# Five edits to a hybrid encoder trunk: unnormalised prompt rows, values stored whole, values between the chunks, gates loaded ahead of the merge

## The chip, the cores and the metric

One core of one Trainium2 chip runs the whole program. The metric is the device time of one launch in microseconds (us), the median of several runs. Times of single instructions come from one profiled execution, taken by the hardware profiler. The engines are TensorE (PE, matmuls; PEld is its weight load), VectorE (DVE), ScalarE (ACT), GpSimd (POOL) and SyncE (SP, which here issues every DMA, in order).

## The reference

One layer and a final norm, applied with the same weights to 512 prompt rows and 1024 sample rows of width 1024, in f32:

```
h = rms_norm(x, norm1_g)
z = h @ w_in                                   # branches and gates
br_a = conformer_conv(z_a)    br_b = multiscale_pool(z_b)    br_c = short_gated_conv(z_c)
br_d = neighbourhood_attention(q, k, v, rpb) @ w_out_d
gates = sigmoid(z_gates + b_gate)              # four gates of width 1024
x = x + (gates0 * br_a + gates1 * br_b + gates2 * br_c + gates3 * br_d) @ w_o
h = rms_norm(x, norm2_g)
x = x + conv_glu_ffn(h, w_up, ffn_conv_w, w_down)
return rms_norm(x, final_g)
```

RMSNorm multiplies each row by the reciprocal of its root mean square (one scalar for each row) and each column by a gain g.

## The kernel before

Activations are kept transposed: features on the 128 partitions, rows along the free axis, in chunks of C = 512 rows. Chunk c = 0 is the prompt, c = 1 and 2 the sample. A row of 1024 features is KT = 8 tiles of 128x512. A product in f32 is made of three matmuls of rounded halves (`mm3`, L121 to L125: high times high, high times low, low times high); `split` (L114, L115) makes the halves, the high one on ACT, the low one on DVE.

**Phase A** (L327 to L531) loads x, and makes the queries and keys (`zt`, four PSUM tiles a chunk) and the values (`zv`, four blocks `b` of 128 rows a chunk, `value_tile`). For the prompt the q/k and values are made from unnormalised rows `raw0` (x times gain), and the row scale goes in at eviction. For the sample `scale(c)` makes the row scale from the sum of squares (matmuls with `ones`, L142, then a small Newton chain on DVE, then the tile `dg`), `spread` (L156) spreads it over the partitions into `rb`, and `norm(k, c)` (L421) multiplies x by it, tile by tile. After q/k of both chunks come the values of chunk 1, with `operands(b)` (sums and differences of sample tiles T1 to T4, on DVE and POOL, stored to DRAM, for a Strassen-like product later), and the values of chunk 2. Between these last value blocks the prompt is loaded a second time (L338), multiplied by gain and row scale `rbp` (L529) and split into `h[0]`.

**Phase B** (L535 to L803) makes the branch projections (`ftile`: tiles `z2_1` for item 2 and chunk 1, and so on, chunk order 1, 2, 0) in a planned order; an attention task list (`bg`) is pumped between them. An attention `step` (24 of them: 2 head pairs, 3 row blocks, 4 column blocks `j`) loads its values `vv`, computes scores, softmax and `o`. Eviction functions `ev_...` take each z from PSUM.

**Gate phase** (L808 to L955): 16 pairs of gate columns, seven products a pair for the sample plus two for the prompt (`plain`), sigmoid, and a store to `gate_d` in DRAM. A side task (`step`, `tick`, TAPS = 5) runs the 31-tap convolution on DVE. At the end `load_bs(c)` loads the branch outputs of chunk c from DRAM (8 tiles `bs` of 128x512) and splits them into `bh` and `bl`.

**Merge** (L963 to L989): for feature tile d and chunk c, `merge(d, c, w)` loads a gate tile of 1 MB (`g`, L970), makes four products `y{d}{c}{i}` (6 matmuls each), multiplies each by its gate on DVE (L975), adds the four on POOL (L976, L977) and DVE (L978). The first two d are interleaved: (0,0), (1,0), (0,1), (1,1), (0,2), (1,2). Eight PSUM banks hold the y tiles.

A scheduler lays all of it out once, when the program is built, by priorities and due times; each engine then runs its own list in order and waits on semaphores. The output projection, the FFN and the final norm follow the merge and are not touched.

## Time and profile before

| what | value |
|---|---|
| median of 3 runs | 2275.09 us (2274.45 to 2275.87) |
| the profiled execution | 2275.41 us |
| its span, first to last instruction | 2273.6 us (1.81 us lie outside) |
| PE busy | 2199.9 us, 97% |
| DVE, ACT, POOL busy | 59%, 34%, 28% |
| mean granted TensorE clock | 0.983 of full speed |

The span less PE's busy time is 73.7 us: the idle time of PE in the whole program. A busy PE at the lower of its two clock levels (granted clock 0.50, which is 1.2 GHz against 2.4 GHz) takes twice as long for a matmul, so the rows carry the granted clock beside the busy time. "[3.83 <-DVE dg L147]" behind an instruction says that its engine had been idle for 3.83 us and that the DVE instruction of line 147, writing `dg`, released it.

### The profile page before, as it was taken

To read this page: it belongs to the slowest core of one execution; us is meant where nothing else is said; L and a number is where in the kernel's file an instruction comes from. 1 tells how busy PE (TensorE), PEld (TensorE's weight loads), DVE (VectorE), ACT (ScalarE), POOL (GpSimd) and SP (SyncE) were. 2 spreads that over 40 slices of the span, in tenths; PEclk is the share of its full clock that TensorE was granted. 3 is DMA by queue.
4 is the path that set the end of the run, shared out by engine and by line. 5 is a ranking of instruction groups with operands and counts; after the bars stand their busy time and mean duration, and the time that the engine had idled before them with its cause. 6 is when DMAs were issued, how large, how long until landed. Compare 5 with 4: busy or idle time off the path is not lost.

```text
span 2273.6 us, 26886 instructions
## 1 busy us (share of the span) xinstructions
PE 2199.9 (97%) x9898; PEld 1789.9 (79%) x9898; DVE 1351.8 (59%) x1946; ACT 781.3 (34%) x1328; POOL 632.4 (28%) x695
## 2 busy tenths in 40 slices
PE   8979999999999999799998999999999999999997
PEld 6767677888888887588786788888888888888886
DVE  6733554436555564677439897778878875341414
ACT  5325444333333333501223533333333333321112
POOL 3201424222222221144234353444444430000001
PEclk9999999999999999899999999999999999999999
DMA  6565232622233223775332321111111114532231
GB/s 214 183 219 175 90 115 68 229 88 93 88 103 102 83 80 111 243 248 194 116 122 101 120 75 61 58 59 65 65 62 60 65 66 167 174 119 59 77 92 51
DMA packets 115444, 259.13 MB, mean 114 GB/s; under 512 B 13168, under 2 KB 23920, under 8 KB 112240
## 3 DMA queue, kind: packets, MB, share of 16 engines
q1 hardware_dynamic: 115312, 257.41, 33.9%
q8 instruction: 78, 1.28, 0.2%
q14 instruction: 54, 0.44, 0.1%
HBM read 169.53 MB, written 87.83 MB: 113 GB/s over the span
## 4 chain that ended last, share of the span: by engine, by line
PE 49%; DVE 2%; issue 0%; POOL 0%; POOLq 0%; ACT 0%; DVEq 0%; ACTq 0%
PE yp L124 5%; PE yp L123 5%; PE yp L125 5%; PE ppu L125 3%; PE ppu L123 3%; PE ppu L124 3%; PE o L124 2%; PE o L123 2%; PE o L125 2%; PE p3T L125 1%; PE p3T L124 1%; PE p3T L123 1%; PE p1T L124 1%; PE p1T L125 1%; PE p1T L123 1%; PE p22T L125 1%
## 5 line engine op out<-in xcount | busy, mean ns | idle before, releaser
L123 PE MATMUL yp<-fs,wdhi 128*128 128x512 f32 x480 | 187.0, 391 | 0.0
L124 PE MATMUL yp<-fs,wdhi 128*128 128x512 f32 x480 | 186.9, 389 | 0.0
L125 PE MATMUL yp<-fs,wdlo 128*128 128x512 f32 x480 | 186.8, 389 | 0.0
L115 DVE TENSOR_TENSOR fs<-fr,fs 128x512 fp32r<-128x512 f32 x63 | 43.5, 691 | 181.8 <-ACT fs L114 181.7
L1173 POOL TENSOR_TENSOR u<-u,u 128x512 f32<-128x512 f32 x63 | 97.5, 1548 | 193.3 <-DVE u L1166 135.6
L123 PE MATMUL z<-hh,wh_i 128*128 128x512 f32 x288 | 120.1, 418 | 11.8 <-ACT hh L114 11.8
L837 DVE SCALAR_TENSOR_TENSOR acc<-glu,pt,acc 128x1552 f32<-128x1552 f32 x60 | 124.2, 2069 | 5.1 <-ACT acc L835 4.2
L124 PE MATMUL z<-hl,wh_i 128*128 128x512 f32 x288 | 116.4, 405 | 0.5 <-DVE hl L115 0.5
L125 PE MATMUL z<-hh,wl_i 128*128 128x512 f32 x288 | 115.7, 403 | 0.0
L1266 POOL TENSOR_TENSOR x<-x,rs 128x256 f32<-128x256 f32 x11 | 7.6, 723 | 366.1 <-DVE acc L1254 362.5
L114 ACT CAST fs<-fr 128x512 fp32r<-128x512 f32 x63 | 39.1, 621 | 199.0 <-DMA fr<-f_d 101.3
L123 PEld LDWEIGHTS yp<-fs,wdhi 128*128 128x128 f32 x480 | 90.1, 188 | 19.5 <-issue 0.5
L124 PEld LDWEIGHTS yp<-fs,wdhi 128*128 128x128 f32 x480 | 90.1, 188 | 19.0 <-issue 0.5
L125 PEld LDWEIGHTS yp<-fs,wdlo 128*128 128x128 f32 x480 | 90.1, 188 | 18.9
L1166 DVE SCALAR_TENSOR_TENSOR u<-c,pt,u 128x512 f32<-128x512 f32 x88 | 100.5, 1180 | 0.0
L123 PE MATMUL y<-bh,wh_wo 128*128 128x512 f32 x192 | 75.8, 395 | 16.2 <-DVE g L975 16.2
L614 POOL TENSOR_TENSOR bm<-R,pt 128x384 f32<-128x384 f32 (+1 forms) x48 | 47.3, 990 | 151.5 <-DVE mx L621 124.4
L1165 DVE SCALAR_TENSOR_TENSOR u<-c,pt,u 128x512 f32<-128x512 f32 x88 | 87.0, 1027 | 0.0
L253 POOL TENSOR_TENSOR Sg<-wr_g,wr_g 128x512 f32<-128x512 f32 x16 | 22.0, 1376 | 217.9 <-DVE Sg1s L115 217.9
L1172 ACT ACTIVATE u<-u 128x512 f32<-128x512 f32 x66 | 41.8, 633 | 111.9 <-DVE u L1166 111.9
L123 PEld LDWEIGHTS z<-hh,wh_i 128*128 128x128 f32 x288 | 55.3, 192 | 28.9 <-ACT hh L114 13.7
L124 PE MATMUL o<-ml,wh_o 128*128 128x512 f32 x192 | 75.6, 394 | 1.2 <-DVE ml L115 1.2
(498 smaller groups left out, 6493.7 us busy)
## 6 DMA issues: line engine op xcount, KB each, us to landing
g<-gate_d SPq DMA_DIRECT2D x24, 1024.0 KB, 5.2
wr_u<-in_w_up SPq DMA_DIRECT2D x44, 512.0 KB, 3.5
f_d<-u SPq DMA_DIRECT2D x66, 256.0 KB, 2.0
fr<-f_d SPq DMA_DIRECT2D x66, 256.0 KB, 2.7
wr_g<-in_w_in SPq DMA_DIRECT2D x32, 512.0 KB, 4.1
wdr<-in_w_dn SPq DMA_DIRECT2D x23, 512.0 KB, 3.5
x<-in_xT SPq DMA_DIRECT2D x32, 256.0 KB, 5.1
gate_d<-gp SPq DMA_DIRECT2D x32, 256.0 KB, 2.9
```

The lines of the kernel that those rows point to most:

```text
L114: S.copy(hi, src)
L115: V.tensor_tensor(lo, src, hi.bitcast(F32), ALU.subtract)
L123: PE.matmul(ps, w[0][:, ws], x[0], start=first, stop=False, **kw)
L124: PE.matmul(ps, w[0][:, ws], x[1], start=False, stop=False, **kw)
L125: PE.matmul(ps, w[1][:, ws], x[0], start=False, stop=last, **kw)
L253: G.tensor_tensor(t, x, y, op)
L614: G.tensor_tensor(bmv, rv, cm[:, None, :].broadcast_to([P, nk, 32]), ALU.add)
L837: keep(V.scalar_tensor_tensor(a, g, w, a, ALU.mult, ALU.add))
L1165: V.scalar_tensor_tensor(b, r[:, 0:C], pc("fc", f * 3), b, ALU.mult, ALU.add)
L1166: V.scalar_tensor_tensor(b, r[:, 2 : C + 2], pc("fc", f * 3 + 2), b, ALU.mult, ALU.add)
L1172: S.activation(ug, ug, AF.Silu)
L1173: (V if j == NJ - 1 else G).tensor_tensor(uv, uv, ug, ALU.mult)
```

## The change

1. The prompt stays unnormalised: `h[0]` is `raw0`. The second load of the prompt, its norm (8 DVE instructions at L529) and its 8 splits go. The row scale `rbp` (now in a pool that lives on) goes in at the eviction of each prompt tile instead.
2. The values of a block are stored by one DMA of 128 partitions, where 8 of 32 partitions were: 12 stores in place of 96. A step's `vv` is then loaded by four DMAs of 32 partitions, where one was: 96 in place of 24.
3. Values of chunk 1 stand between the q/k of chunk 1 and of chunk 2; the spread of chunk 2's row scale comes after value block 2 and its first two norms after block 3. `operands(b)` stand with the values of chunk 2.
4. The loads of `bs` for chunks 1 and 2 move behind the gate phase, into a pool of 4 tiles of their own, and the first three gate tiles (0,0), (1,0), (0,1) are loaded among them.
5. The gate pool has 9 tiles, and the sums S1 to S4 of the gate weights come from it, where they came from the T pool (TPN 34 to 32, TPA 40 to 39). The loop that ran the rest of the side task empty becomes an assertion; TAPS stays 5.

```diff
-            raw0 = {}
+            raw0 = [None] * KT
+            h[0] = raw0
...
-                    raw0[k] = hl(f"rh{k}"), hl(f"rl{k}")
+                    raw0[k] = pr[k] = hl(f"rh{k}"), hl(f"rl{k}")
...
-                for r in range(2):
-                    for j in range(4):
-                        lo = r * GW + CB[j]
-                        SP.dma_start(vt_d[j, c * 8 + b * 2 + r], o[lo : lo + 32, :].bitcast(F32))
+                SP.dma_start(vt_d[2 * (c * 4 + b) : 2 * (c * 4 + b) + 2].rearrange("r c d -> (r c) d"), o.bitcast(F32))
...
             for c in (1, 2):
+                zz = [ztile(f"zt{c}{n}") for n in range(4)]
...
                 for b in range(4):
                     value_tile(c, b, h[c])
-                    if c == 1:
+                    if c == 1 and b == 2:
+                        spread(*stat[2][:2])
+                    if c == 1 and b == 3:
+                        with tc.high_priority():
+                            norm(0, 2)
+                            norm(1, 2)
+                    if c == 2:
                         operands(b)
-                    else:
-                        for k in (2 * b, 2 * b + 1):
-                            load_x(k, 0)
-                            keep(V.scalar_tensor_tensor(x[k, 0], x[k, 0], pc("g1", k), rbp, ALU.mult, ALU.mult))
-                            h[0][k] = pr[k] = hl(f"hh{k}_0"), hl(f"hl{k}_0")
-                            split(*h[0][k], x[k, 0])
...
-                        SP.dma_start(
-                            vv[:, :nt].bitcast(F32),
...
+                        for r in range(4):
+                            SP.dma_start(
+                                vv[r * 32 : (r + 1) * 32, :nt].bitcast(F32),
...
                     def ev_g(c, z):
                         sig[c] = go(f"sig{i}{c}")
+                        if c == 0:
+                            V.tensor_tensor(sig[c], z, rbp, ALU.mult)
+                            z = sig[c]
                         S.activation(sig[c], z, AF.Sigmoid)
+                        if c == 0:
+                            G.tensor_tensor(sig[c], sig[c], rbp, ALU.mult)
...
+                        if c == 0:
+                            V.tensor_tensor(o, z, rbp, ALU.mult)
+                            G.tensor_tensor(o, o, rbp, ALU.mult)
+                        else:
+                            S.copy(o, z)
...
+                        o = cc[:, OFF[0] : OFF[0] + C]
+                        G.tensor_tensor(o, o, rbp, ALU.mult)
...
                     z = prompt(n, s, wg)
-                    gate_out(*gate, 0, z, go(f"gp{s}{n}"))
+                    o = go(f"gp{s}{n}")
+                    V.tensor_tensor(o, z, rbp, ALU.mult)
+                    gate_out(*gate, 0, o, o)
...
             for _ in step:
-                pass
-            load_bs(1)
-            load_bs(2)
+                raise AssertionError
...
+                    bst = pool(p2a, "bst", 4, side="right")
+                    load_gate(0, 0)
+                    load_bs(1)
+                    load_gate(1, 0)
+                    load_gate(0, 1)
+                    load_bs(2)
```

Where the instructions stand now. **First place, PE after the q/k of chunk 1**, where the row scale of chunk 2 is made (`rb0_2`; `zt2.` are q/k of chunk 2, `zv1.` and `zv2.` values). Before:

```order
L142 MATMUL rb0_2_874<-ones_168,sq0_24_812 128x1
L156 MATMUL rb0_2_874<-dg0_2_875,ones_168 128x512
L123 MATMUL zt20_924<-hh0_2_929,wh_q0_186 128x512
L123 MATMUL zt21_925<-hh0_2_929,m0h0_259 128x512
L123 MATMUL zt22_926<-hh0_2_929,wh_k0_189 128x512
L123 MATMUL zt23_927<-hh0_2_929,m1h0_277 128x512
L460 MATMUL zv10_1088<-vwh0_316,hh0_1_645 128x256
```

After:

```order
L142 MATMUL rb0_2_849<-ones_168,sq0_24_787 128x1
L463 MATMUL zv10_898<-vwh0_320,hh0_1_627 128x256
...
L465 MATMUL zv12_956<-vwh3_323,hl7_1_830 128x256
L156 MATMUL rb0_2_849<-dg0_2_850,ones_168 128x512
L463 MATMUL zv13_986<-vwh0_320,hh0_1_627 128x256
...
L465 MATMUL zv13_986<-vwh3_323,hl7_1_830 128x256
L123 MATMUL zt20_1025<-hh0_2_1016,wh_q0_190 128x512
L123 MATMUL zt21_1026<-hh0_2_1016,m0h0_263 128x512
```

Three value blocks (72 matmuls of 256 columns) now stand between the sum of squares and the spread, and one (24) between the spread and the first product of chunk 2.

**Second place, SP at the end of phase A**: the value stores (`vt_d`), the second load of the prompt (`x0_0` and on), the operand stores (`t_d`) and the first loads of phase B (`wr_i3`, `qh0`). Before:

```order
L519 DMA t_dT43_119<-T4l3_1342 128x512
L473 DMA vt_d_103<-vs20_1373 32x512 x8
L338 DMA x0_0_1384<-in_xT 128x512
L338 DMA x1_0_1391<-in_xT 128x512
L473 DMA vt_d_103<-vs21_1423 32x512 x8
...
L338 DMA x7_0_1541<-in_xT 128x512
L202 DMA wr_i3_1668<-in_w_in 128x1024
L202 DMA wr_i4_1765<-in_w_in 128x1024
L656 DMA qh0_1755<-qh_d0_95 128x1536
```

After:

```order
L473 DMA vt_d_103<-vs22_1320 128x512
...
L473 DMA vt_d_103<-vs23_1378 128x512
L497 DMA t_dT13_107<-T1l3_1388 128x512
...
L497 DMA t_dT43_119<-T4l3_1406 128x512
L202 DMA wr_i3_1533<-in_w_in 128x1024
L202 DMA wr_i4_1630<-in_w_in 128x1024
L650 DMA qh0_1620<-qh_d0_95 128x1536
```

The prompt loads are gone, a value block is one row where it was eight, and the operand stores of the last tiles stand right ahead of the phase B loads.

**Third place, DVE at the start of the merge** (`bl` is the low half of a branch tile, `g00` the gate tile of d = 0, c = 0, multiplied by the products `y`). Before:

```order
L115 TENSOR_TENSOR wl_wo1_7807<-wr_wo1_7805,wh_wo1_7806 128x1024
L115 TENSOR_TENSOR bl001_7703<-bs001_7700,bh001_7702 128x512
L115 TENSOR_TENSOR bl011_7709<-bs011_7706,bh011_7708 128x512
...
L115 TENSOR_TENSOR bl312_7793<-bs312_7790,bh312_7792 128x512
L975 TENSOR_TENSOR g00_7819<-y000_7821,g00_7819 128x512
```

After:

```order
L115 TENSOR_TENSOR wl_wo1_7791<-wr_wo1_7789,wh_wo1_7790 128x1024
L999 TENSOR_TENSOR g00_7687<-y000_7803,g00_7687 128x512
L999 TENSOR_TENSOR g00_7687<-y001_7811,g00_7687 128x512
L999 TENSOR_TENSOR g00_7687<-y002_7819,g00_7687 128x512
L115 TENSOR_TENSOR bl001_7692<-bs001_7689,bh001_7691 128x512
L999 TENSOR_TENSOR g00_7687<-y003_7827,g00_7687 128x512
L115 TENSOR_TENSOR bl011_7698<-bs011_7695,bh011_7697 128x512
L115 TENSOR_TENSOR bl101_7704<-bs101_7701,bh101_7703 128x512
L1002 TENSOR_TENSOR m0_7801<-g00_7687 128x512
L115 TENSOR_TENSOR bl111_7710<-bs111_7707,bh111_7709 128x512
L999 TENSOR_TENSOR g10_7737<-y100_7838,g10_7737 128x512
```

All 16 low halves stood ahead of the first gate product; now the gate products come first and the low halves between them. SP's list at this place, before:

```order
L818 DMA gate_d7_64<-gr15_7697 128x512
L890 DMA bs001_7700<-bs_d001_121 128x512
...
L890 DMA bs312_7790<-bs_d312_143 128x512
L970 DMA g00_7819<-gate_d0_57 128x2048
L970 DMA g10_7856<-gate_d1_58 128x2048
```

After:

```order
L828 DMA gate_d7_64<-gr15_7672 128x512
L982 DMA g00_7687<-gate_d0_57 128x2048
L902 DMA bs001_7689<-bs_d001_121 128x512
L902 DMA bs011_7695<-bs_d011_124 128x512
L902 DMA bs101_7701<-bs_d101_127 128x512
L902 DMA bs111_7707<-bs_d111_130 128x512
L982 DMA g10_7737<-gate_d1_58 128x2048
L902 DMA bs201_7713<-bs_d201_133 128x512
...
L902 DMA bs311_7731<-bs_d311_142 128x512
L982 DMA g01_7739<-gate_d0_57 128x2048
L902 DMA bs002_7741<-bs_d002_122 128x512
```

The first gate load stands right behind the last gate store, and each later `bs` load reuses the slot of the fourth `bs` load before it.

## Rows read from the trace of the kernel before

**Rows 1.** PE's waits: engine, line, waited for: us in total, times, longest us

```profile
PE y L123 <- DVE g L975: 16.2, 1, 16.2
PE z L123 <- ACT hh L114: 11.8, 3, 10.1
PE rb L156 <- DVE dg L147: 6.8, 3, 3.8
PE tp L633 <- ACT se L630: 4.1, 10, 0.7
```

**Rows 2.** Windows: us, PE PEld DVE ACT POOL busy (instructions), PEclk, DMA share, GB/s

```profile
85.00:90.00 5.00, 3.92 (x14) 3.54 (x15) 5.00 (x9) 2.47 (x4) 1.28 (x1) 0.50 0.07 25
150.00:200.00 50.00, 43.20 (x169) 32.12 (x170) 18.56 (x35) 15.76 (x26) 3.23 (x7) 0.83 0.76 253
250.00:300.00 50.00, 48.86 (x246) 35.49 (x244) 23.60 (x65) 25.80 (x59) 19.84 (x21) 1.00 0.36 122
450.00:500.00 50.00, 50.00 (x223) 41.39 (x222) 19.83 (x23) 20.14 (x31) 10.99 (x7) 1.00 0.30 88
955.00:960.00 5.00, 3.35 (x8) 2.71 (x9) 3.27 (x6) 0.00 (x0) 2.52 (x2) 0.50 0.97 408
1220.00:1225.00 5.00, 3.12 (x14) 2.04 (x12) 5.00 (x6) 1.24 (x2) 4.92 (x3) 1.00 0.22 64
```

**Rows 3.** Timeline at chunk 2's row scale, PE then DVE: start, us, instruction [idle before]

```profile
82.51 2.08 PE L156 MATMUL rb<-dg,ones 128*128 128x512 f32 x2 [3.83 <-DVE dg L147]
86.08 0.80 PE L123 MATMUL zt<-hh,wh_q 128*128 128x512 f32 x1 [1.49 <-ACT hh L114]
91.58 0.30 PE L462 MATMUL zv<-vwh,hl 128*128 128x256 f32 x1
91.71 0.28 PE L460 MATMUL zv<-vwh,hh 128*128 128x256 f32 x1
84.62 5.36 DVE L421 SCALAR_TENSOR_TENSOR x<-x,pg,rb 128x512 f32<-128x512 f32 x8 [1.57 <-PE rb L156]
119.33 0.68 DVE L115 TENSOR_TENSOR T4l<-x,T4h 128x512 fp32r<-128x512 f32 x1
```

**Rows 4.** Timeline at the first projections, PE, DVE, SP

```profile
133.45 0.40 PE L123 MATMUL z<-hh,wh_i 128*128 128x512 f32 x1
154.58 0.80 PE L123 MATMUL z<-hh,wh_i 128*128 128x512 f32 x1 [10.06 <-ACT hh L114]
185.70 0.39 PE L123 MATMUL z<-hh,wh_i 128*128 128x512 f32 x1
153.13 0.75 DVE L529 SCALAR_TENSOR_TENSOR x<-x,pg,rbp 128x512 f32<-128x512 f32 x1 [18.65 <-DMA x<-in_xT]
146.22 4.04 SPq L473 DMA_DIRECT2D vt_d<-vs  x8
```

**Rows 5.** Timeline at the start of the merge, PE, DVE, SP

```profile
940.04 0.39 PE L125 MATMUL y<-bh,wl_wo 128*128 128x512 f32 x1
956.65 0.77 PE L123 MATMUL y<-bh,wh_wo 128*128 128x512 f32 x1 [16.23 <-DVE g L975]
939.37 5.38 DVE L115 TENSOR_TENSOR bl<-bs,bh 128x512 fp32r<-128x512 f32 x8 [8.50 <-ACT bh L114]
933.08 12.02 SPq L890 DMA_DIRECT2D bs<-bs_d  x16
950.70 14.15 SPq L970 DMA_DIRECT2D g<-gate_d  x5
```

**Rows 6.** DMA issues from 905 to 980 us: instruction, count, KB each, median us to landing

```profile
g<-gate_d SPq DMA_DIRECT2D x8, 1024.0 KB, 5.3
bs<-bs_d SPq DMA_DIRECT2D x23, 256.0 KB, 4.3
```

**Rows 7.** Attention stage, 190 to 450 us: a value load; POOL's and ACT's instructions by line

```profile
vv<-vt_d SPq DMA_DIRECT2D x16, 384.0 KB, 3.2
L614 POOL TENSOR_TENSOR bm<-R,pt 128x384 f32<-128x384 f32 x32 | 33.0, 1034 | 79.8 <-DVE mx L621 79.8
```

More of the change, by code (lines that the diff above doesn't have):

```diff
@@ L42 @@
 TAPS = 5
-TPA = 40
-TPN = 34
+TPA = 39
+TPN = 32
 NBIG = 9
@@ L325, in tt @@
             return tp.tile([P, C], dt, tag="t", name=name)
+        rbp = pool(outer, "rbp", 1).tile([P, C], F32, name="rbp")
         with ExitStack() as pha:
@@ L729, in ev_gc @@
                             t["gc"] = big(f"gc{i}")
-                        S.copy(t["gc"][:, ch(c)], z)
+                        o = t["gc"][:, ch(c)]
+                        if c == 0:
+                            V.tensor_tensor(o, z, rbp, ALU.mult)
+                            G.tensor_tensor(o, o, rbp, ALU.mult)
+                        else:
+                            S.copy(o, z)
                     def ev_xv(c, z):
@@ L785, in encoder @@
                 early = Weights([(w_in[idx], f"i{idx}") for idx, _ in todo])
-                wg = PairWeights("g", lambda n: tuple(w_in[gate_idx(*g)] for g in pairs[n]), lambda name: tt(name))
+                wg = PairWeights("g", lambda n: tuple(w_in[gate_idx(*g)] for g in pairs[n]), lambda name: go(name))
                 left = len(todo)
@@ L810, in encoder @@
             cvp = pool(phb, "cvp", 2, side="right")
-            go1 = pool(phb, "gob", 8, side="right")
+            go1 = pool(phb, "gob", 9, side="right")
             def go(name, dt=F32):
@@ L888, in load_bs @@
                     for k in range(2):
-                        t = go(f"bs{i}{k}{c}")
+                        t = bst.tile([P, C], F32, tag="go", name=f"bs{i}{k}{c}")
                         SP.dma_start(t, bs_d[i, k, c])
@@ L965, in encoder, with load_gate @@
                     gp = pool(p2a, "gp", 3, side="right")
-                    merged = []
+                    merged, gate = [], {}
+                    def load_gate(d, c):
+                        gate[d, c] = gp.tile([P, 4, C], F32, tag="g", name=f"g{d}{c}")
+                        SP.dma_start(gate[d, c], gate_d[d][:, c])
+                    bst = pool(p2a, "bst", 4, side="right")
[4 more added lines that the diff above has]
+                    load_bs(2)
                     def merge(d, c, w):
-                        g = gp.tile([P, 4, C], F32, tag="g", name=f"g{d}{c}")
-                        SP.dma_start(g, gate_d[d][:, c])
+                        if (d, c) not in gate:
+                            load_gate(d, c)
+                        g = gate[d, c]
                         for i in range(4):
```

50 lines of the change are left out of this document (22 added, 28 removed).

## The prediction

> **What bounds the kernel now.** I read PE's waits first, then the windows, then the timelines of the places that the waits name. PE is busy for 2199.9 of 2273.6 us, so a change that leaves its work alone can win two things: the 73.7 us in which it is idle, and the time that it runs at its lower clock. From 450 to 500 us it is full: 223 matmuls of 512 columns in 50 us, 0.224 us each [rows 2]. Three waits stand out, and all three are at places that the change touches: 16.2 us for the first gate product, 11.8 us for the prompt's high halves, and 6.8 us for `dg`, of which 3.8 us are at chunk 2's row scale [rows 1]. The clock adds to them: behind each, the granted clock is 0.50, as from 85 to 90 us and from 955 to 960 us [rows 2]. It need not fall after every gap: from 1220 to 1225 us PE was busy for 3.12 of 5 us and the clock stayed at 1.00 [rows 2]. DVE, ACT and POOL are half idle or more in most stages, so work added to them counts only where PE waits for it.
>
> **The change, place by place.** The order of PE has 9709 instructions in both programs; what moves is what it waits for.
>
> *Place A, the row scale of chunk 2.* Before, PE ended the sums at 82.51 - 3.83 = 78.68 us, was idle for 3.83 and 1.49 us [rows 3], and ran from 82.51 to about 91.6 us at the lower clock (9.1 us less 1.49 idle: 7.6 us for work of 3.8). Lost: 5.3 + 3.8 = 9.1 us. Now three value blocks, 72 matmuls of 0.12 to 0.13 us (91.58 to 91.71 [rows 3]), follow the sums and last until 87.4 us; `dg` was there at 82.5 us, so the spread waits for nothing. The eight norms on DVE then take their 5.36 us [rows 3], from some 88.3 to 93.7 us, and the low half comes at 94.4 us, since DVE's order has it behind all eight. PE has value block 3 (24 matmuls, 2.9 us), four q/k and eight value products with the high half (1.9 us): until 92.7 us. So 1.7 us of idle stay, less than the case in which the clock held. Gain: 9.1 - 1.7 = 7.4 us; the first projection moves from 133.45 us [rows 4] to 126.1 us. Bounds: 4 us, if the clock falls after all (2.5 us more) and the operand chain (rival 1) is a little late; 9 us, if nothing waits.
>
> *Place B, the first projections.* Six projection tiles (144 matmuls) stand from 133.45 to 185.70 us [rows 4], 52.2 us for 144 x 0.224 = 32.3 us of work. The 10.06 us wait [rows 4] is DVE's for the second load of the prompt (18.65 us [rows 4]); it sits on SP behind value stores of 0.5 us each (8 in 4.04 us [rows 4]), and the three further blocks of 8 between its pairs make the smaller waits that follow and, with them, a clock of 0.83 on average from 150 to 200 us [rows 2]. Now `h[0]` is the raw prompt, made in the first microseconds of the program, and there is no load to wait for: 52.2 - 32.3 = 19.9 us. What is late next is `q0`, `k0`, `R0` for the first attention step. SP has 25 issues of about 0.5 us after the last chunk 2 query (121.5 us by my walk along the order), so these loads start at some 138 us and land by 155 us (3.6 MB at the 253 GB/s of this stretch [rows 2] take 14 us; I take 17); the scores are reached at 126.1 + 38 = 164 us. Bounds: 17 to 20 us.
>
> *Place C, the start of the merge.* Before, the gates were issued behind 16 `bs` loads (12.02 us, then the wait for slots until 950.70 [rows 5]), a gate takes 5.3 us to land [rows 6], and DVE's first product released PE at 956.65 us, 16.23 us idle [rows 5]; half clock behind it for some 5 us costs 2.4 us. The 96 matmuls of the tiles y010 to y123 then last 96 x 0.224 = 21.5 us: until 956.65 + 2.4 + 21.5 = 980.6 us. Now `g00` is issued at 933.1 us and lands at 938.4 us, before PE ends its first 48 matmuls (940.3 us). Then DVE is the pace: for each chunk 8 gate products, 8 low halves and 2 sums, 18 x 0.65 = 11.7 us (8 low halves took 5.38 us [rows 5]). Chunk 1's last low half comes at 938.5 + 11.7 = 950.2 us or, with the slot chain, 951 us; chunk 2's 11.7 us later, 962 to 963 us; some 20 matmuls (4.5 us) follow it: 967.5 us. Gain: 980.6 - 967.5 = 13 us, less 1 us for a clock that may fall in the broken stretch: 12 us. Bounds: 7 us (rival 2) and 15.5 us (DVE packs perfectly from 938.5 us and the clock holds).
>
> *Attention stage, 190 to 450 us.* New are 6 DVE products of 0.68 us (a low half of that size took 0.68 [rows 3]), four of them in place of ACT copies; 6 POOL products of about 1.4 us (1.03 us at 384 columns [rows 7], scaled to 512); and 72 more issues of about 0.4 us on SP, 30 of 260 us. PE is nearly full there (48.86 of 50 us from 250 to 300 us [rows 2]) and its only steady wait is for the softmax, 4.1 us in ten pieces [rows 1]. A POOL product ahead of a bias tile `bm` can delay a step by 1.4 us, six times at most. DVE and POOL are under half busy, so most hides. I take 1.5 us; bounds -1 and 8 us.
>
> *Gate phase.* 32 DVE products of 0.68 us (22 us over 450 us, DVE busy for 19.83 of 50 [rows 2]) come between a prompt product and its sigmoid. PE's order is unchanged but for pair 0, and a PSUM tile is read by DVE where ACT read it. I take 0; bounds 0 and 3 us. The sums S1 to S4 in gate tiles have one slot more and wait for stores that are long done: 0.
>
> *"Six taps a pair".* The code has no such edit: TAPS is 5 before and after, and 15 pairs of 5 cover the side task either way. 0.
>
> Sum: 7.4 + 19.9 + 12 - 1.5 = 37.8 us. From the profiled execution's 2275.41 us that is 2237.6 us; that execution stands 0.3 us above the median. The operand chain has no slack at the first projection (rival 1), for which I add 1.5 us: **2239 us**.
>
> **Rivals.** *1. The operand chain becomes the bound.* `operands(b)` now run on DVE, ACT and POOL behind chunk 2's norms. Before, the last T4 low half came at 119.33 us [rows 3], four rounds of 6 us from about 92 us; now they begin at some 96 us and end at 122 us or later, and behind them on DVE stand the low halves of chunk 2's keys and values, whose banks the first projection needs, at 126.1 to 128.4 us by my walk. For: PE reaches the projection at 126.1 us, so there is no slack. Against: the chain's pieces on PE's list are two tiles further on. If it is 4 us late and the clock falls for 5 us, 6.5 us are lost: about 2245.5 us, and with half of rival 2, 2248 us.
>
> *2. The merge is a chain of slots.* With four `bs` slots a load waits for the low half of the fourth before it: 0.4 issue + 4.3 landing [rows 6] + 0.6 + 0.7 split = 6 us for four pieces, 24 us for sixteen, and each of the three gates of 1 MB among them may add 3 us in the same queues (the DMA share was 0.97 at 408 GB/s once the gates ran [rows 2]): 933.5 + 24 + 9 = 966.5 us, then 4.5 us of matmuls and 2.5 us of clock: 973.5 us. The gain at C is 7 us: 2244 us.
>
> *3. Slower: the narrow value loads.* A step's values are loaded two steps ahead into two buffers: once `o` of a step is done, the load for the step after next may start, and one step (260 / 24 = 10.8 us) covers it. One load of 384 KB lands in 3.2 us [rows 7]. If the four quarters run one after the other at the same 3.2 us each, they take 12.8 + 1.2 us and PE waits 3.2 us in each of 24 steps: 77 us, some 2316 us. It decides from a chain of 10.8 us on; the gain is used up at 10.8 + 37.8 / 24 = 12.4 us. Against: 16 `bs` loads of 256 KB were issued every 0.75 us and landed in 4.3 us each [rows 5, 6], so loads overlap, and four quarters should be there after 1.2 + 3.2 = 4.4 us. The Trainium skill (DMA: Bandwidth & Descriptors, "Rules for kernel authors") speaks against this edit: it says that two transfers to disjoint halves of the partitions serialize, and that one transfer of 128 partitions is better. No row of before shows a load split like this. By that rule the quarters would share the engines and take as long as the whole, and this rival would need them to take three times as long.
>
> *4. Nothing moves.* It would need waits of the same size behind each of the three places; no row shows such a one.
>
> **How the numbers follow.** Forecast, 2231 to 2247 us: 0.70. Rivals 1 and 2, alone or together, 2244 to 2256 us: 0.23. Rival 3, in full or as a like loss in another stage: 0.05 (above 2280 us). No change: 0.02. The best sum is 9 + 20 + 15.5 + 1 = 45.5 us, 2230 us; the worst without rival 3 is 4 + 17 + 7 - 11 = 17 us, 2258 us, which needs every bound at once, so I stop at 2254 us. A measurement of this kernel tells 0.2% (4.5 us) from no change. Faster by more: 0.93; within: 0.02; slower: 0.05.
>
> **What would show it.** In the profile of the changed kernel: A, no wait for `dg` at chunk 2's scale and one wait below 2 us for a low half, granted clock 1.00 from 80 to 95 us. B, no wait of `z` for `hh`, the six tiles in 32 to 33 us and a clock of 1.00 from 125 to 160 us. C, no wait for the first gate product above 1 us, several of 0.5 to 2 us for low halves between 940 and 963 us of the old time scale. Attention, PE's share as before. The prediction is wrong if `z` waits for `ksl` or `vs` by over 4 us, if scores wait for the q/k loads, if `o` waits for `vv`, or if one wait at the merge stays above 6 us.

## The result, and the profile after

The changed kernel took **2248.49 us** (median of 4 runs, 2248.18 to 2251.82) where the kernel before took 2275.48 us on the same chip (2274.45 to 2278.62, 4 runs): a ratio of 0.9882, 95% interval 0.9865 to 0.9900. The predicted range, 2230 to 2254 us, holds it, and faster was the likeliest side; the predicted time, 2239.0 us, was 9.5 us too low. The profiled execution took 2248.36 us with a span of 2246.6 us, so 27.05 us less than the one of before.

PE does the same work. The first line is the page's busy time by engine, to be held against the 2199.9 us of before:

```profile
PE 2198.7 (98%) x9898; PEld 1789.2 (80%) x9898; DVE 1358.8 (60%) x1968; ACT 775.7 (35%) x1316; POOL 614.0 (27%) x701
```

PE's waits after, in the columns of [rows 1]:

```profile
PE y L124 <- DVE bl L115: 5.5, 4, 1.7
...
PE tp L627 <- ACT se L624: 2.6, 7, 0.6
PE yp L123 <- ACT fs L114: 2.6, 1, 2.6
...
PE y L123 <- DVE g L999: 1.8, 1, 1.8
...
PE zv L463 <- DVE x L424: 1.2, 1, 1.2
```

The 16.2 us for the first gate product are 1.8 us; the 11.8 us of `z` for `hh` are gone; at chunk 2's scale one wait of 1.2 us is left. Two of size are new: 5.5 us for the low halves at the merge, and 2.6 us for `fs`, far away in the down products of the feed-forward stage. The windows after, in the columns of [rows 2] (the first three around places A and B, the next three at the merge, the last at the start of the down products):

```profile
50.00:100.00 50.00, 47.41 (x273) 40.69 (x272) 33.46 (x63) 18.77 (x36) 8.07 (x6) 1.00 0.33 124
...
100.00:150.00 50.00, 50.00 (x265) 43.25 (x264) 29.53 (x38) 18.11 (x30) 15.32 (x11) 1.00 0.76 286
150.00:200.00 50.00, 50.00 (x242) 38.69 (x241) 15.61 (x56) 23.30 (x49) 10.65 (x14) 1.00 0.45 154
```

```profile
915.00:920.00 5.00, 2.67 (x6) 1.89 (x7) 5.00 (x7) 2.47 (x4) 2.73 (x2) 0.61 0.79 295
920.00:925.00 5.00, 3.41 (x8) 1.84 (x7) 5.00 (x7) 1.85 (x3) 1.45 (x2) 0.71 0.70 222
925.00:930.00 5.00, 4.82 (x12) 3.16 (x13) 5.00 (x8) 1.59 (x3) 1.65 (x1) 0.66 0.84 292
...
```

```profile
1880.00:1890.00 10.00, 9.01 (x32) 7.02 (x33) 5.69 (x7) 4.27 (x7) 0.00 (x0) 0.83 0.75 262
```

From 100 to 200 us PE has no idle time and its clock is 1.00, where before, from 150 to 200 us, it was busy for 43.20 of 50 us at 0.83 [rows 2]. At the merge DVE is busy for the whole of each of the three windows and PE's clock is 0.61 to 0.71; in the first two of them PE also waits.

To see where the time went, both programs are cut at the first matmul of a stage: `zt` from the sample's halves `hh` (queries and keys), `z` (first projection), `s` (scores), `yg` (gate phase), `y` from `bh` (merge), `o` from the merged rows `mh` (output projection), `ppu` (feed-forward up), `yp` with the second half's weights `wdhi3` and on (down). A stage's length is the difference of two such starts, which are read to 0.1 us; the last ends with the execution.

| stage | before, us | after, us | gain | predicted gain |
|---|---|---|---|---|
| start to `zt` | 52.9 | 54.1 | -1.2 | 0 |
| `zt` to `z` (place A) | 80.5 | 73.3 | 7.2 | 7.4 |
| `z` to `s` (place B) | 57.8 | 38.2 | 19.6 | 19.9, and -1.5 for the operand chain |
| `s` to `yg` (attention) | 246.2 | 246.4 | -0.2 | -1.5 |
| `yg` to `y` (gate phase) | 492.0 | 491.0 | 1.0 | 0 |
| `y` to `o` (place C) | 149.5 | 144.9 | 4.6 | 12 |
| `o` to `ppu` | 147.4 | 146.5 | 0.9 | 0 |
| `ppu` to `yp` | 683.6 | 686.3 | -2.7 | 0 |
| `yp` to the end | 365.5 | 367.7 | -2.2 | 0 |
| sum | | | 27.0 | 36.3 |

The start is no part of the change: over all kernels of this study, none of which edits it, the first `zt` matmul came between 52.8 and 57.1 us. What is left to explain is 7.4 us at place C and 4.9 us in the last two rows.

### The profile page after: what moved, and what is told of

Same layout as the page of the kernel before. It is cut to its first block, busy times and chain, and to the rows that moved or that the text cites. A ratio compares the mean times of both kernels' runs of the same rounds, so it can differ in the third digit from the quotient of the medians.

```text
span 2246.6 us, 26949 instructions
## 1 busy us (share of the span) xinstructions
PE 2198.7 (98%) x9898; PEld 1789.2 (80%) x9898; DVE 1358.8 (60%) x1968; ACT 775.7 (35%) x1316; POOL 614.0 (27%) x701
## 4 chain that ended last, share of the span: by engine, by line
PE 50%; DVE 2%; issue 0%; POOL 0%; ACT 0%; POOLq 0%; DVEq 0%; ACTq 0%
PE yp L124 5%; PE yp L125 5%; PE yp L123 5%; PE ppu L123 4%; PE ppu L125 4%; PE ppu L124 4%; PE o L124 2%; PE o L125 2%; PE o L123 2%; PE p3T L123 1%; PE p3T L124 1%; PE p3T L125 1%; PE p1T L124 1%; PE p1T L125 1%; PE p1T L123 1%; PE p22T L125 1%
## 5 line engine op out<-in xcount | busy, mean ns | idle before, releaser
L253 POOL TENSOR_TENSOR Sg<-wr_g 128x512 f32<-128x512 f32 x16 | 21.2, 1327 | 329.6 <-DMA wr_g<-in_w_in 329.6
L847 DVE SCALAR_TENSOR_TENSOR acc<-glu,pt,acc 128x1552 f32<-128x1552 f32 x60 | 109.8, 1830 | 0.4
L124 PE MATMUL y<-bl,wh_wo 128*128 128x512 f32 x192 | 77.5, 404 | 5.6 <-DVE bl L115 5.5
L123 PE MATMUL z<-hh,wh_i 128*128 128x512 f32 x192 | 78.3, 408 | 0.0
L125 PE MATMUL z<-hh,wl_i 128*128 128x512 f32 x192 | 76.5, 398 | 0.0
L124 PE MATMUL z<-hl,wh_i 128*128 128x512 f32 x192 | 76.4, 398 | 0.0
```

Source lines behind the costliest of these rows:

```text
L123: PE.matmul(ps, w[0][:, ws], x[0], start=first, stop=False, **kw)
L124: PE.matmul(ps, w[0][:, ws], x[1], start=False, stop=False, **kw)
L125: PE.matmul(ps, w[1][:, ws], x[0], start=False, stop=last, **kw)
L253: G.tensor_tensor(t, x, y, op)
L847: keep(V.scalar_tensor_tensor(a, g, w, a, ALU.mult, ALU.add))
```

## Experiments

### The four parts alone

Four kernels put one part of the change each into the kernel before. e1_raw_only takes the moves of part 5 with it (the weight sums in gate tiles, a gate pool of 9), and e2_store_only changes the value stores and the value loads together.

**e1_raw_only: the raw prompt with the scale at eviction.**

```
-            raw0 = {}
+            raw0 = [None] * KT
+            h[0] = raw0
...
-                    raw0[k] = hl(f"rh{k}"), hl(f"rl{k}")
+                    raw0[k] = pr[k] = hl(f"rh{k}"), hl(f"rl{k}")
...
-                        for k in (2 * b, 2 * b + 1):
-                            load_x(k, 0)
-                            keep(V.scalar_tensor_tensor(x[k, 0], x[k, 0], pc("g1", k), rbp, ALU.mult, ALU.mult))
-                            h[0][k] = pr[k] = hl(f"hh{k}_0"), hl(f"hl{k}_0")
-                            split(*h[0][k], x[k, 0])
...
-                        S.copy(t["xb"][:, OFF[c] : OFF[c] + C], z)
+                        o = t["xb"][:, OFF[c] : OFF[c] + C]
+                        if c == 0:
+                            V.tensor_tensor(o, z, rbp, ALU.mult)
+                        else:
+                            S.copy(o, z)
...
```

> The kernel before with part 1 alone (raw prompt kept, scale at eviction; the weight sums in gate tiles as part 5 has them, since the T pool has no room otherwise); values still stored by 96 narrow DMAs. If the second load of the prompt alone made the 19.5 us of place B, the six projection tiles run without a gap and the time is 2275 - 19.5 + 5 (the wait at the start of the FFN's second half, which the shifted tile slots should bring here too) = 2260.5 us. Rival: the 96 stores on SP still stand ahead of the loads of q, k and the rel table; these would be issued at some 164 us and land at some 178 to 180 us, while the scores are due at 171 us, so 8 us of the gain go into a new wait: 2268 us.

**e2_store_only: a value tile stored in one piece, a value load in four.**

```
-    vt_d = dram("vt_d", [4, T // GW, 32, 4 * P])
+    vt_d = dram("vt_d", [T // GW, GW, 4 * P])
...
-                for r in range(2):
-                    for j in range(4):
...
+                SP.dma_start(vt_d[2 * (c * 4 + b) : 2 * (c * 4 + b) + 2].rearrange("r c d -> (r c) d"), o.bitcast(F32))
...
+                        for r in range(4):
+                            SP.dma_start(
+                                vv[r * 32 : (r + 1) * 32, :nt].bitcast(F32),
...
```

> The kernel before with part 2 alone (a value block in one store, four narrow value loads a step); the prompt is still loaded and normed a second time. If the queue of 96 stores ahead of the prompt loads was the cause of place B, and not the second load as such, the prompt loads are issued by some 130 us, the projections of the prompt find their halves ready, and most of the 19.5 us are won: 2256 to 2259 us. If the second load itself is the cause, the wait of z for hh stays above 5 us and the time stays at 2272 to 2275 us. The four narrow loads a step cost nothing in either case: o waits for vv nowhere.

**e3_values_only: chunk 1's value tiles ahead of chunk 2's queries and keys.**

```
...
                 for b in range(4):
                     value_tile(c, b, h[c])
-                    if c == 1:
+                    if c == 1 and b == 2:
+                        spread(*stat[2][:2])
+                    if c == 1 and b == 3:
+                        with tc.high_priority():
+                            norm(0, 2)
+                            norm(1, 2)
+                    if c == 2:
                         operands(b)
...
```

> The kernel before with part 3 alone (values of chunk 1 between the chunks, operands with the values of chunk 2). Place A gains its 7.3 us: no wait for dg at chunk 2's scale and the clock at 1.00 from 80 to 95 us. If the places are independent, 2268 us. Rival: the operand stores now stand on SP between the prompt loads, place B's wait grows by what A won, and the time stays within 3 us of 2275.

**e4_gates_only: the first gates ahead of the `bs` loads, in four slots of their own.**

```
...
-            load_bs(1)
-            load_bs(2)
             tstack.close()
...
+                    bst = pool(p2a, "bst", 4, side="right")
+                    load_gate(0, 0)
+                    load_bs(1)
+                    load_gate(1, 0)
+                    load_gate(0, 1)
+                    load_bs(2)
...
```

> The kernel before with part 4 alone (three gate tiles loaded ahead, bs in four slots of their own). In the changed kernel the start of the merge was worth 4.7 us, of 12 forecast. If that is the edit's own size, 2270 us here, with the same broken waits for bl, y's single wait for g below 3 us, and low halves of 1.4 to 1.7 us beside POOL's adds. If the changed kernel's other parts held it back (its gate phase ends with other stores in flight), the gain here is 8 us or more: below 2267 us.

Measured beside a kernel before of 2277.75 us, with the stage lengths of one profile each:

| kernel | us, median (n) | ratio, 95% interval | A | B | attention | C | `ppu` to `yp` |
|---|---|---|---|---|---|---|---|
| before | | | 80.5 | 57.8 | 246.2 | 149.5 | 683.6 |
| e1_raw_only | 2266.67 (7) | 0.9947, 0.9928 to 0.9965 | 80.7 | 42.9 | 250.9 | 147.8 | 687.0 |
| e2_store_only | 2260.26 (4) | 0.9913, 0.9891 to 0.9935 | 79.2 | 41.3 | 246.1 | 148.6 | 683.6 |
| e3_values_only | 2270.91 (10) | 0.9967, 0.9954 to 0.9980 | 73.3 | 58.6 | 246.3 | 149.4 | 683.3 |
| e4_gates_only | 2273.69 (10) | 0.9981, 0.9967 to 0.9996 | 80.8 | 58.0 | 246.4 | 145.5 | 683.2 |
| changed | | | 73.3 | 38.2 | 246.4 | 144.9 | 686.3 |

Each place answers to its part: A belongs to the value tiles alone (7.2 us), C to the gates alone (4.0 us of the 4.6; its profile, 2278.24 us, is the longest of its ten runs, with a gate phase of 494.7 us, 1.1 us of which are a longer wait for a load of `accn`). Place B has two parts that each remove most of the same loss: 14.9 us by the raw prompt, 16.5 us by the single store, 19.6 us together. So it was a queue, narrow stores with prompt loads behind them, and either end of it could be cut. (In e2_store_only, which took 2260.26 us where 2256 to 2259 were expected, 1.1 us of waits of `z` for `hh` are left.) The narrow stores had a second victim, which the raw prompt alone leaves in place. PE's waits from 130 to 430 us in e1_raw_only:

```profile
PE tp L629 <- ACT se L626: 3.8, 7, 1.3
PE z L123 <- ACT wh_i L114: 1.7, 1, 1.7
PE z L125 <- DVE wl_i L115: 0.5, 1, 0.5
PE s L601 <- DMA kh<-kh_d: 0.4, 1, 0.4
```

Weights (`wh_i`, and with them `wl_i`) and keys (`kh`) come late there: 2.6 us, all of it between the first projection at 135.3 us and the first score at 178.2 us. The new wait of 8 us at the scores that its rival expected is 0.4 us. Its attention takes 4.7 us more than before, but not by such waits. In the same stretch behind the first score, e1_raw_only and then the kernel before:

```profile
218.00:238.00 20.00, 18.16 (x73) 13.48 (x72) 15.94 (x28) 5.41 (x12) 5.33 (x7) 0.83 0.15 46
231.00:251.00 20.00, 18.16 (x79) 11.88 (x78) 15.95 (x33) 7.88 (x17) 9.14 (x10) 1.00 0.29 92
```

PE is busy for the same 18.16 us, but behind a softmax wait of 1.3 us at 230 us its clock falls in the one and not in the other, where the longest such wait is 0.7 us [rows 1]; 0.17 of 20 us are 3.4 us of the 4.7. What makes that wait longer, and whether the late loads have a part in it, no run shows, and it is one profile.

And 3.4 us of the loss ahead of `yp` are in e1_raw_only and in none of the other three: that loss belongs to the raw prompt (or to the moves that go with it, below), a thousand microseconds after its last use.

**e11_undo_store: the changed kernel with the narrow stores put back.** Its edit is that of e2_store_only, reversed.

> The changed kernel with the value stores put back into 96 narrow ones (and the value loads into 24 whole ones). Theory: the queue of narrow stores stands between the value phase and the query and key loads again; with prompt rows that no longer wait for their second load only a part of it is covered, so the middle stage (first value matmul to first score matmul) takes about 43 us instead of 38.2 and the attention some 4 to 5 us more for late loads, as in e1_raw_only: about 2258 (2254 to 2262). Rival: with the value tiles now between the chunks the narrow stores spread over a longer time and are drained before the prompt; then the stages stay at 38.2 and 246.4 and the time within 2 us of the changed kernel.

One execution took 2263.76 us, more than the range expected. Place B takes 48.3 us instead of some 43, the attention 246.9 us instead of 250 or more: of the 15.4 us above the changed kernel 10.1 us are in place B, and hardly any in the attention. In the timeline, PE's wait (start, us, instruction, idle before, and what released it), then ACT's, then the issues on SP's queue:

```profile
158.06 0.80 PE L123 MATMUL z<-hh,wh_i 128*128 128x512 f32 x1 [7.35 <-ACT sig L672]
```

```profile
156.12 1.28 ACT L672 ACT_TABLE_LOAD   x1 [26.79 <-DMA t_dT<-T1h]
```

```profile
141.04 4.05 SPq L476 DMA_DIRECT2D vt_d<-vs  x8
...
149.80 4.05 SPq L476 DMA_DIRECT2D vt_d<-vs  x8
153.90 0.43 SPq L503 DMA_DIRECT2D t_dT<-T1h  x1
```

SP issues without a gap here; eight narrow stores hold it for 4.05 us, and the store of `T1h` stands behind them. The sigmoid `sig` waits for that store, and a projection tile of PE waits for the sigmoid: 7.35 us, and the dozen matmuls behind it start 0.43 us apart where the later ones are 0.23 us apart (1.9 times; the granted clock is 0.50 from 158 to 163 us). So what the narrow stores cost is SP's issue time, 0.5 us each, and whoever is next in that queue pays. The expected victims (query and key loads) were not the ones; the queue was.

### The late loss: `ppu` to the end

In the changed kernel, ACT at the start of the down products (timeline, columns as above), and PE beside it:

```profile
1878.09 1.99 ACT L114 CAST wdhi<-wdr 128x1024 fp32r<-128x1024 f32 x2 [9.35 <-PE yp L125]
1879.99 1.66 ACT L114 CAST fs<-fr 128x512 fp32r<-128x512 f32 x3
```

```profile
1880.65 1.20 PE L123 MATMUL yp<-fs,wdhi 128*128 128x512 f32 x4 [2.60 <-ACT fs L114]
1882.19 0.80 PE L124 MATMUL yp<-fs,wdhi 128*128 128x512 f32 x1 [0.34 <-DVE fs L115]
```

and the same cast in the kernel before:

```profile
1900.65 1.99 ACT L114 CAST wdhi<-wdr 128x1024 fp32r<-128x1024 f32 x2
```

Before, the first weights of the second half are cast as soon as ACT is free, some nine microseconds before PE wants them. After, the cast waits 9.35 us for a product of PE, because its buffer lies where two weight tiles of the early down products lie: in the placement of the compiled program the first of these casts, `wdhi3`, takes the bytes 65088 to 69184 of a partition in both programs, and `wdlo20` and `wdlo21`, last read by the last early products (line 125 of PE), stand at 56896 to 60992 before and at 65088 to 69184 in the changed kernel and in e1_raw_only. Without the sixteen halves of the prompt, other slots are free when these two tiles ask for one; part 5's moves alone, compiled with the kernel before and not run, leave both at 56896 to 60992. e1_raw_only shows the same wait (9.35 us of ACT, 2.6 us of PE). The test changes the placement alone: the pool of the weights is opened ahead of the pool of the residual rows, so that `wdhi3` shares its bytes with `fh00` and `fl00`, which are read first of all.

**e5_ffn_pools**

```
-        x3p = pool(p4, "x3p", 4)
         wdb = pool(p4, "wdb", NJ - 2)
+        x3p = pool(p4, "x3p", 4)
```

> The changed kernel, with two pools of the FFN's second half opened in the other order (the weight pool before the pool of loaded rows), so that the first weight tile of that half no longer lies over tiles that the third of the early products still reads. The changed kernel waits 2.6 us there and runs some 5 us at half clock; neither program of the diff names this place. If the shift of tile slots by the 16 prompt halves that are no longer made is the cause, the wait of yp for fs goes, the stage from the first up product to the first down product takes 683.5 us (686.3 in the changed kernel) and the down products 330.3 us (332.5): 5 us less, 2243.5 us. If the wait is only a late transfer of one run, both stages keep their lengths here or had them shorter by chance: within 1 us of the changed kernel.

Measured: 2242.68 us (2240.42 to 2246.41, n = 4) against 2279.51 us of before on that chip, ratio 0.9844, 95% interval 0.9827 to 0.9862 (the changed kernel: 0.9882, 0.9865 to 0.9900). `ppu` to `yp` is 683.6 us again and the down stage as before. Its casts and the window that answers to 1880 to 1890 us above:

```profile
1868.08 1.03 ACT L114 CAST wdhi<-wdr 128x1024 fp32r<-128x1024 f32 x1
1869.02 0.61 ACT L114 CAST fs<-fr 128x512 fp32r<-128x512 f32 x1
1869.54 1.05 ACT L114 CAST wdhi<-wdr 128x1024 fp32r<-128x1024 f32 x1
```

```profile
1880.00:1890.00 10.00, 10.00 (x45) 8.27 (x45) 4.38 (x5) 4.29 (x5) 0.00 (x0) 1.00 0.86 304
```

The cast is 10 us earlier, PE is full and its clock 1.00. This loss of 4.9 us (2.7 ahead of `yp`, 2.2 behind it) is shown: it came with the raw prompt and goes with the placement.

### The merge

DVE at the merge of the changed kernel, two rounds of one gate tile each, then POOL's sums in the same stretch (timelines):

```profile
914.53 1.89 DVE L999 TENSOR_TENSOR g<-y,g 128x512 f32<-128x512 f32 x3 [9.87 <-PE y L125]
916.33 1.52 DVE L115 TENSOR_TENSOR bl<-bs,bh 128x512 fp32r<-128x512 f32 x1
917.78 0.68 DVE L999 TENSOR_TENSOR g<-y,g 128x512 f32<-128x512 f32 x1
918.38 2.36 DVE L115 TENSOR_TENSOR bl<-bs,bh 128x512 fp32r<-128x512 f32 x2
920.66 0.68 DVE L1002 TENSOR_TENSOR m<-g 128x512 f32<-128x512 f32 x1
921.26 0.68 DVE L115 TENSOR_TENSOR bl<-bs,bh 128x512 fp32r<-128x512 f32 x1
921.87 1.87 DVE L999 TENSOR_TENSOR g<-y,g 128x512 f32<-128x512 f32 x3
```

```profile
916.04 1.27 POOL L1000 TENSOR_TENSOR g<-g 128x512 f32<-128x512 f32 x1 [23.55 <-DMA bs<-bs_d]
918.54 1.65 POOL L1001 TENSOR_TENSOR g<-g 128x512 f32<-128x512 f32 x1 [1.23 <-DMA g<-gate_d]
```

A low half takes 0.68 us when POOL is still, and 1.52 us when it meets a sum: it starts at 916.33, POOL's sum ends at 917.31, and it ends 0.54 us later, at 917.85. Of the pair at 918.38 the first starts ahead of POOL's second sum, and POOL's takes 1.65 us instead of 1.27; the other ends at 920.74, again 0.55 us after POOL's end at 920.19. Gate products, of which one operand is in PSUM, keep their 0.68 us beside sums. Those of the kernel before from 955 to 982 us, with POOL's sums running between and beside them (count, then shortest, median and longest in ns, first and last start):

```profile
L975 DVE TENSOR_TENSOR g<-y,g x24: 675/682/692, 955.8 to 981.2; 128x512 f32<-128x512 f32 x24
L976 POOL TENSOR_TENSOR g<-g x6: 1281/1293/1303, 957.3 to 980.8; 128x512 f32<-128x512 f32 x6
```

The Trainium skill (SBUF — State Buffer, "Who interferes with whom") says that a VectorE instruction with two SBUF inputs contends with a GpSimd instruction that reads SBUF, and that the port pair which they share is an exclusive lock. The times above agree: whichever starts second is the longer one.

Three kernels change one thing each: e6_no_adds leaves POOL's two sums out of the first six merged tiles (two of their four products are missing there), e7_eight_slots gives every `bs` load of a chunk its own slot, and e8_bs_first also issues four `bs` loads ahead of the first gate.

**e6_no_adds**

```
-                        G.tensor_tensor(g[:, 0], g[:, 0], g[:, 1], ALU.add)
-                        G.tensor_tensor(g[:, 2], g[:, 2], g[:, 3], ALU.add)
+                        if d > 1:
+                            G.tensor_tensor(g[:, 0], g[:, 0], g[:, 1], ALU.add)
+                            G.tensor_tensor(g[:, 2], g[:, 2], g[:, 3], ALU.add)
```

> The changed kernel without the two GpSimd adds for feature tiles 0 and 1 of the merge: two of four gate products are left out of the first six merged tiles. Theory: in the start of the merge VectorE is the pace, and its low halves (two operands in SBUF) take 1.4 to 1.7 us in place of 0.69 while GpSimd adds. Then without the adds every low half takes 0.69 us, the round of VectorE for one gate tile falls from 7.3 to 5.9 us, and the stage of y takes 140 to 142 us (144.9 in the changed kernel, 149.5 before). Rival: the four slots and the landings of bs are the pace; then VectorE idles where it was slow, the rounds stay at 7 us and the stage at 144 to 145 us.

**e7_eight_slots**

```
-                    bst = pool(p2a, "bst", 4, side="right")
+                    bst = pool(p2a, "bst", 8, side="right")
```

> The changed kernel with eight bs slots in place of four. The scheduler then issues all eight loads of chunk 1 ahead of the second gate tile. If the chain of slots held the start of the merge back, the waits of y for bl fall below 3 us in all (5.5 us in the changed kernel) and the stage of y takes 141 us or less. If VectorE is the pace, the waits move but the stage stays within 1.5 us of 144.9 us.

**e8_bs_first**

```
-            def load_bs(c):
-                for i in range(4):
+            def load_bs(c, rows=range(4)):
+                for i in rows:
...
-                    bst = pool(p2a, "bst", 4, side="right")
+                    bst = pool(p2a, "bst", 8, side="right")
+                    load_bs(1, (0, 1))
                     load_gate(0, 0)
-                    load_bs(1)
+                    load_bs(1, (2, 3))
                     load_gate(1, 0)
+                    load_bs(2, (0, 1))
                     load_gate(0, 1)
-                    load_bs(2)
+                    load_bs(2, (2, 3))
```

> The changed kernel with eight bs slots and four bs loads issued ahead of the first gate tile. VectorE was idle for 9.9 us until the first gate tile landed at 914.5 us; here it can make four low halves in that time, with no GpSimd add beside them, and the first gate tile lands some 2.5 us later behind 1 MB more. If VectorE's work is the pace, the stage of y takes 140 to 142 us although PE waits 2 to 3 us longer for the first gate product. If the landing of the gates is the pace, the stage takes 146 to 148 us.

One execution each: 2245.44, 2241.97 and 2245.95 us; the stage takes 140.6, 140.1 and 141.8 us instead of 144.9. In e6_no_adds a round of DVE is 5.41 us instead of 7.34 (913.48 to 918.89 and 914.53 to 921.87), with every low half at 0.68 us, and then DVE stands still for the next gate:

```profile
913.48 1.89 DVE L999 TENSOR_TENSOR g<-y,g 128x512 f32<-128x512 f32 x3 [9.44 <-PE y L125]
...
917.69 1.29 DVE L115 TENSOR_TENSOR bl<-bs,bh 128x512 fp32r<-128x512 f32 x2
918.89 1.88 DVE L999 TENSOR_TENSOR g<-y,g 128x512 f32<-128x512 f32 x3
...
926.31 1.89 DVE L999 TENSOR_TENSOR g<-y,g 128x512 f32<-128x512 f32 x3 [1.62 <-DMA g<-gate_d]
```

In e7_eight_slots the low halves no longer come one by one as slots free, so fewer of them meet a sum (the 16 take 13.7 us in all, not 18.0), and PE waits 3.0 us for them instead of 5.5. In e8_bs_first four of them stand ahead of the first gate product at 0.69 us each, but most of the others meet a sum again (16.3 us in all); PE waits 1.0 us for low halves and 6.8 us for gates that were issued later. So DVE's pace beside POOL, the chain of four slots and the landing of the gates all press on these 30 us; taking one away leaves the next. Single executions do not rank the three.

### Both remedies together

**e9_pools_slots** has the edits of e5_ffn_pools and e7_eight_slots.

> The changed kernel with both remedies: the down weights' pool opened before the pool of the residual rows (as in e5_ffn_pools) and eight slots for the low rows of the merge (as in e7_eight_slots). Theory: the two losses sit in different stages and add up, so the merge stage (first merge matmul to first output projection) takes about 140 us instead of 144.9, the down stage keeps 330.3 us from first to last matmul instead of 332.5, and the time is 2242.7 - 4.5 = about 2238 (2235 to 2241). Rival: the four-slot chain and the VectorE pace are one loss that the later output projection takes back; then the time is that of e5_ffn_pools, about 2242.7.

**e10_pools_slots_dve** has them too, and

```
-                        G.tensor_tensor(g[:, 0], g[:, 0], g[:, 1], ALU.add)
-                        G.tensor_tensor(g[:, 2], g[:, 2], g[:, 3], ALU.add)
+                        E = V if d < 2 else G
+                        E.tensor_tensor(g[:, 0], g[:, 0], g[:, 1], ALU.add)
+                        E.tensor_tensor(g[:, 2], g[:, 2], g[:, 3], ALU.add)
```

> As e9_pools_slots, and the sums over the pairs of gate rows of the first two passes go to VectorE instead of GpSimd. Theory A (GpSimd beside VectorE is what stretches the low halves): every low half takes about 0.7 us instead of 1.4 to 1.8, but VectorE takes over two sums of some 0.7 us a gate tile, so the merge stage is within 1.5 us of e9_pools_slots. Theory B (the low halves are slow by themselves): they stay at 1.4 to 1.8 us and the stage grows by about 1.4 us a gate tile, some 8 to 11 us in all, to about 150 us and 2248.

Beside a kernel before of 2279.67 us: e9_pools_slots took 2241.64 us (2237.93 to 2242.87, n = 5), ratio 0.9834, 95% interval 0.9818 to 0.9850; e10_pools_slots_dve took 2239.56 us (2236.30 to 2242.78, n = 4), ratio 0.9829, 0.9812 to 0.9847. Both beat the changed kernel's 0.9882; between the two, and against e5_ffn_pools, the intervals overlap. In the profiles the merge is 140.1 us in e9_pools_slots and 137.8 us in e10_pools_slots_dve (e5_ffn_pools: 143.9). By form, the low halves from 905 to 950 us in the changed kernel and in e10_pools_slots_dve (count, busy us, mean ns, idle before):

```profile
L115 DVE TENSOR_TENSOR bl<-bs,bh 128x512 fp32r<-128x512 f32 x16 | 18.0, 1145 | 0.0
```

```profile
L115 DVE TENSOR_TENSOR bl<-bs,bh 128x512 fp32r<-128x512 f32 x16 | 10.8, 692 | 0.0
```

Theory A of that run holds: with POOL still, all 16 take 0.69 us. DVE's sums cost 0.69 us each, 1.4 us a round, and POOL's had cost more than that in low halves (7.34 less 5.41 us a round, above). The stage is 2.3 us shorter than in e9_pools_slots, where theory A expected it within 1.5 us. e9_pools_slots came out 0.6 us above its expected span of times: the down stage and the merge are as expected (330.3 and 140.1 us), but its output projection (`o` to `ppu`) takes 149.3 us, against 146.9 in e5_ffn_pools and 146.6 in e10_pools_slots_dve, with a lower clock towards its end. The windows of e9_pools_slots and e10_pools_slots_dve:

```profile
1160.00:1190.00 30.00, 28.48 (x118) 22.96 (x117) 22.73 (x49) 9.69 (x17) 8.38 (x6) 0.89 0.25 77
```

```profile
1160.00:1190.00 30.00, 25.85 (x116) 20.50 (x116) 25.94 (x51) 10.30 (x18) 12.97 (x8) 0.97 0.27 88
```

PE's waits in that stage are the same in both (2.6, 1.5 and 1.2 us), so why the clock was lower in one of them stays open, and with one profile each, whether it always is.

## Why the prediction was right, and where its steps were off

*Place A* was right in mechanism and size. 7.2 us were won, 7.4 predicted; e3_values_only shows that part 3 does it alone. The spread of the scale stands among the value products without a wait:

```profile
88.39 0.28 PE L465 MATMUL zv<-vwh,hl 128*128 128x256 f32 x1
88.51 1.02 PE L156 MATMUL rb<-dg,ones 128*128 128x512 f32 x2
88.97 0.68 PE L463 MATMUL zv<-vwh,hh 128*128 128x256 f32 x1
```

The one remaining wait was put at 1.7 us, for a low half; it is 1.2 us, of a value product for the last of the eight norms. The clock held, as taken. (The prediction counts 9709 instructions on PE; both pages have 9898. That the two programs have the same number holds.)

*Place B* was right: 19.6 of 19.9 us, no wait of `z` for `hh`, PE full from 100 to 200 us. Its mechanism was told as one part's work (no load to wait for); e1_raw_only and e2_store_only show that the store in one piece would have won most of it too (16.5 us), and that without it the raw prompt wins 14.9 us and leaves 2.6 us of waits for weights and keys. *Rival 1*, the operand chain, did not come: PE waits for neither `ksl` nor `vs`, and the 1.5 us set aside for it were not needed.

*Attention and rival 3.* The stage changed by 0.2 us where 1.5 us were taken, and PE never waits for `vv`: in e2_store_only too it takes 246.1 us. The quarters of 96 KB of a value load (by DMA issue: count, KB, median us to landing), in the changed kernel:

```profile
vv<-vt_d SPq DMA_DIRECT2D x63, 96.0 KB, 2.2
```

A whole one took 3.2 us [rows 7]; a quarter takes 2.2 us, and with issues 0.5 to 1.4 us apart (3 in 1.50 us from 240.11, 5 in 7.19 us from 231.75) all four are there inside one step of 10.8 us. The Trainium skill's advice against splitting (DMA: Bandwidth & Descriptors, "Rules for kernel authors") does not bind here: the loads have two steps of lead, and what the split buys, one store instead of eight, is on a queue that had none to spare.

*Gate phase:* 1.0 us gained where 0 was taken (an earlier wait of 1.3 us for a load of `accn` is gone).

*Place C* is the term that was mis-sized: 12 us predicted with bounds of 7 and 15.5, 4.6 us won, below the lower bound; its sign, no wait above 1 us for the first gate product, failed too (1.8 us). Two steps of its working failed. The gate `g00`, issued at 907.30 us, was given 5.3 us to land, a median of the stretch before [rows 6]; ahead of it in the queues now stand a weight load and stores, the DMA share is 1.01 from 910 to 915 us, and gates and `bs` loads from 900 to 925 us land in

```profile
g<-gate_d SPq DMA_DIRECT2D x3, 1024.0 KB, 7.2
bs<-bs_d SPq DMA_DIRECT2D x8, 256.0 KB, 5.3
```

so DVE starts at 914.53 us and not at 912.6: 1.9 us. The trace of before had a row for this place: behind the same weight load and stores, the first eight `bs` loads, a quarter of a gate's size, took 5.0 to 5.6 us to land; and of its gates, those issued right behind another took 7.1 and 9.1 us. Which of the loads ahead makes the difference, no run separates. And DVE was given 18 x 0.65 = 11.7 us a chunk, with a low half at the 0.67 us of [rows 5], where POOL was still. The 16 low halves of two chunks took 18.0 us instead of 10.8, and from DVE's first product to the last low half there are 30.0 us (914.53 to 944.5) instead of the 24.5 worked out (938.5 to 963): 5.5 us. 1.9 + 5.5 = 7.4 us is what was missing. That they meet it to the tenth is in part luck: on the time scale of before `g00` was also issued 0.6 us later than taken (933.7), and the matmuls behind the last low half took some 1 us more than the 4.5, against the 1 us that was set aside for the clock. With POOL's sums and the four slots both out of the way the stage takes 137.8 us (e10_pools_slots_dve), where the forecast of 12 us would have made it 137.5. The clock, put at 1 us, was 0.61 to 0.71 for 15 us besides; that its cost is already in these figures is how I read it, not a thing that a run separates. *Rival 2* named the chain of slots for such a loss; it is part of the cause (e7_eight_slots), but the row that would have shown the other part, a low half beside a sum of POOL, was not in what the prediction read: before, the low halves ran ahead of the gates.

*What no step spoke of* is the loss of 4.9 us at the down products. The prediction followed what each part does in its own stage and the queues; that taking away sixteen tiles moves the addresses of others, and that a reused address is a wait, was not among its steps. Without it the changed kernel would have stood at some 2243.5 us (2248.4 - 4.9), within 4.5 us of the forecast. That the range held although place C fell below its bound and this loss was not foreseen is in part luck: 4.7 us went the other way (1.5 for the operand chain and 1.3 in the attention that were set aside and not needed, 1.0 in the gate phase and 0.9 in the output projection that nobody forecast).

## What to carry to other kernels

When a change takes tiles away or adds some, read PE's waits in the stages that it does not touch: a tile that lands on bytes still in use waits for their last reader, and the order in which pools are opened can undo that for nothing. When work is moved beside other work, price it from rows in which that neighbour runs: a VectorE instruction with both operands in SBUF is not the same instruction beside GpSimd. A loss that sits in a queue can be removed from either end, so two cures of it are not to be added up.

## What the runs showed of the hardware that was not expected

- A 128x512 subtraction of two SBUF operands on DVE took 0.68 us alone, and 1.52 us when it started 0.29 us into a sum on POOL; the product with an operand in PSUM stayed at 0.68 to 0.69 us. The sum on POOL took 1.65 us instead of 1.27 where DVE was first.
- Gate loads of 1 MB landed in 7.2 us (median of three) with other loads ahead of them, the DMA share at 1.01 and 390 GB/s, where 5.3 us was their median before [rows 6], with single ones from 4.8 to 9.1 us.
- Eight narrow stores of 64 KB (their rows overlap) keep SP for 4.05 us; one store of 256 KB replaces them, and the two cures of place B were worth 14.9 and 16.5 us, each alone.
